# The first norm's row copy ahead of the low halves, paired column tiles in the gated feed-forward, and two-matmul products from its fifth group on

## The chip, the cores and the metric

One NeuronCore of a Trainium2 chip runs the whole program. The metric is the device time of one execution in microseconds (us). The kernel before took 830.42 us (median of 3 runs, 828.53 to 830.56). A profile is one further execution on the same kind of core, recorded by the hardware.

Engines: TensorE (PE in the rows; PEld is its weight load), VectorE (DVE), ScalarE (ACT), GpSimd (POOL) and SyncE (SP, here only a DMA queue). Each works through its own instructions strictly in order; an instruction that waits holds up all that stand behind it on that engine.

## The reference

Two layers over 256 positions of width 1024, in float32. Per layer:

```
h = rmsnorm(x)
qkv of three attention branches, gates = split(h @ w_in)
m = sum_i sigmoid(gate_i) * (attention_i(...) @ w_branch[i]);  x += m @ w_out
h = rmsnorm(x)
u = causal depthwise conv3(h @ w_up) + conv_b        # three taps along the positions
x += (silu(u_a) * u_v) @ w_down                      # u_a, u_v: the halves of u, 2816 columns each
```

A last rmsnorm ends it. The attention branches are a sliding window with sinks (A), stick-breaking (B) and a block-sparse one (C).

## The kernel before

**Split operands.** Every float32 operand of a large product is kept as a high half (rounded to the matmul's input format, by an ACT copy, tile `whi` for weights) and a low half (the remainder, by a DVE subtraction, tile `wlo`); `split` (L270) makes both. A product of a 128x128 block of weights with 256 positions is `three` (L351): high x high, high x low, low x high, each 256 columns wide into one PSUM half bank. `two` (L358) does the same work with 2 matmuls: the high half of the weights against both halves of the activations laid side by side (512 columns), then the low half of the weights against the high half of the activations (256 columns). It leaves two sums of 256 columns in the PSUM tile, which someone has to add up.

**Weights.** They come as pieces of 128x2048 (1 MB) by DMA on SP into 4 `raw` buffers and are split in two cuts of 1024 columns (`weights`, L260). There are 6 buffers each for `whi` and `wlo`, so three pieces; ACT can write a high half only once PE has finished with the cut that used the buffer six cuts earlier. One piece holds two column tiles of 128 outputs (f = 0 and 1), one in each cut, with 8 products per tile.

**Norms.** A norm isn't applied to x ahead of the product that needs it. The product starts on x times the gain (tile `xg`), and its results are scaled by 1/rms afterwards. Meanwhile the sum of squares goes through PE (L306), DVE (`var`, L309), POOL (a power, `rn`, L311) and PE again (L318), and DVE copies the result, a row of 256 scales, from PSUM into `rb` (L321). From `rb` DVE makes the scaled activations `hs` (L347, L273, L344), which the products behind use. In the first norm of a layer, q and k of branch B are computed from `xg` and scaled by `rb` (L645, 8 instructions: tiles `blk`, first q and then k); PE reads the last of them for the first logits of branch B (matmuls `at<-blk`).

**Feed-forward.** 11 groups (i = 0 to 10). In each, part a = 0 (towards silu) and part a = 1 (towards the value) take one piece of weights and give two column tiles each: 4 tiles x 8 products. `conv` (L761) makes of each tile's PSUM sum one ACT instruction (bias and the tap of the present position, L769) and two DVE instructions (the other two taps, L770 and L771). Then ACT takes silu, DVE multiplies, and ACT and DVE split the product into the gate tile `gT[i]`, tile by tile. The tiles of group 0 and the first part of group 1 are computed from `xg` and multiplied by `rb` first (L766). PSUM has 4 banks called `at` and 4 called `mm`; part 0 takes two of the first, part 1 two of the second (group 10 takes `at` for both). In layer 0 the down projection then runs output tile by output tile over k = 0 to 21, with k = 20 and 21 read from `gT[10]`; in layer 1 it runs over k outermost, and k = 18 to 21 come last.

**What sets the order.** PE's instructions are issued in the order of the code; side tasks (a norm's small matmuls, the attention) are put between by a clock that adds up columns. The order on ACT, DVE and POOL is set by the scheduler of the framework, which may move instructions past one another. `issue_after` holds an instruction back until another one of the order has been issued. Before, the low halves of the piece for k of branch B (n, c = 1, 0) are held back behind POOL's power in that way.

## Time and profile before

| | |
|---|---|
| runs | 830.42 us median (828.53 to 830.56) |
| profiled execution | 830.54 us, span 828.4 us |
| TensorE busy | 816.3 us, 99% of the span |
| VectorE busy | 670.9 us (81%) |
| ScalarE busy | 537.4 us (65%) |
| granted TensorE clock | 0.997 over the span |
| chain that ended last | PE 90%, DVE 4%, issue 4%, ACT 1% |

The span is what the profiler recorded from the first to the last instruction; the execution's own time is 2.1 us longer. A line of the page that groups instructions gives their total busy time, the mean of one, and the time that the engine stood idle in front of them. A matmul's own duration in a row overlaps its neighbours', so the pace of a row of matmuls is read from their starts.

### The profile page before, as it was taken

How to read it: one execution, taken by the hardware profiler on the slowest of the kernel's cores; microseconds unless marked ns; L12 is line 12 of the kernel's file. 1: busy time of each engine (PE TensorE's matmuls, PEld its weight loads, DVE VectorE, ACT ScalarE, POOL GpSimd, SP SyncE). 2: the span in 40 equal slices, each digit the busy share in tenths (PEclk: the TensorE clock that was granted, in tenths of full speed). 3: DMA queues.
4: the chain of work that ended last, by engine and by line, in shares of the span. 5: the costliest groups of instructions: out<-in, count | busy, mean ns of one | idle time of the engine just before them, and what ended most of it. 6: DMA issues, size and time to landing. Idle time of an engine off the chain costs nothing.

```text
span 828.4 us, 15607 instructions
## 1 busy us (share of the span) xinstructions
PE 816.3 (99%) x6268; PEld 768.9 (93%) x6268; DVE 670.9 (81%) x1205; ACT 537.4 (65%) x892; POOL 14.0 (2%) x17
## 2 busy tenths in 40 slices
PE   8999999999999999999999999999999999999996
PEld 6978899999999999999999889999999999999885
DVE  6878899677699999876658889896668999988543
ACT  7677569565567776665546777686556686766442
POOL 0100000000000000000000000000000100000000
PEclk9999999999999999999999999999999999999999
DMA  9754443555554676555565441544654566555611
GB/s 352 262 198 153 153 154 106 193 197 178 193 187 170 203 230 208 189 195 203 197 203 203 136 170 51 205 154 157 209 200 147 212 217 215 204 199 203 203 51 51
DMA packets 22631, 151.43 MB, mean 183 GB/s; under 512 B 2656, under 2 KB 3424, under 8 KB 4896
## 3 DMA queue, kind: packets, MB, share of 16 engines
q1 hardware_dynamic: 21744, 148.97, 51.3%
q8 instruction: 49, 0.80, 0.4%
q10 hardware_dynamic: 576, 0.69, 0.3%
q0 software_dynamic: 240, 0.79, 0.2%
q14 instruction: 22, 0.18, 0.1%
HBM read 149.39 MB, written 1.05 MB: 182 GB/s over the span
## 4 chain that ended last, share of the span: by engine, by line
PE 90%; DVE 4%; issue 4%; ACT 1%; POOL 0%; POOLq 0%; ACTq 0%
PE mm L181 67%; PE at L181 20%; PE at L185 2%; DVE wlo L273 1%; ACT blk L546 0%; ACT whi L271 0%; DVE blk L645 0%; DVE half L347 0%; POOL gx L217 0%; PE mm L185 0%; POOL rn L311 0%; DVE blk L559 0%; DVE half L396 0%; PE at L318 0%; DVE half L397 0%
## 5 line engine op out<-in xcount | busy, mean ns | idle before, releaser
L273 DVE TENSOR_TENSOR wlo<-raw,whi 128x1024 fp32r<-128x1024 f32 (+1 forms) x291 | 341.0, 1179 | 100.1 <-ACT whi L271 99.5
L271 ACT ACTIVATE whi<-raw 128x1024 fp32r<-128x1024 f32 (+1 forms) x291 | 294.1, 1020 | 169.9 <-PE mm L181 138.8
L181 PE MATMUL mm<-hs,whi 128*128 128x256 f32 (+1 forms) x1152 | 228.1, 294 | 0.0
L181 PEld LDWEIGHTS mm<-hs,whi 128*128 128x128 f32 x1152 | 181.9, 191 | 6.2 <-issue 0.9
L181 PE MATMUL mm<-hs,wlo 128*128 128x256 f32 x672 | 184.3, 274 | 0.0
L181 PE MATMUL mm<-blk,whi 128*128 128x256 f32 (+1 forms) x742 | 166.2, 312 | 0.1
L181 PE MATMUL mm<-blk,wlo 128*128 128x256 f32 x496 | 135.8, 274 | 0.0
L181 PEld LDWEIGHTS mm<-blk,whi 128*128 128x128 f32 x742 | 121.9, 191 | 7.8 <-DVE blk L273 0.6
L181 PEld LDWEIGHTS mm<-hs,wlo 128*128 128x128 f32 x672 | 129.0, 192 | 0.0
L181 PE MATMUL at<-hs,whi 128*128 128x256 f32 x640 | 108.5, 276 | 0.0
L181 PEld LDWEIGHTS at<-hs,whi 128*128 128x128 f32 x640 | 97.0, 192 | 0.0
L181 PEld LDWEIGHTS mm<-blk,wlo 128*128 128x128 f32 x496 | 95.2, 192 | 0.0
L181 PE MATMUL mm<-whi,hs 128*128 128x512 f32 (+1 forms) x320 | 94.7, 369 | 0.0
L181 PE MATMUL at<-hs,wlo 128*128 128x256 f32 x320 | 88.0, 275 | 0.0
L181 PEld LDWEIGHTS mm<-whi,hs 128*128 128x128 f32 x320 | 59.1, 192 | 8.3 <-issue 0.3
L181 PEld LDWEIGHTS at<-hs,wlo 128*128 128x128 f32 x320 | 61.4, 192 | 0.0
L181 PE MATMUL mm<-wlo,hs 128*128 128x512 f32 (+1 forms) x160 | 57.9, 362 | 0.0
L181 PE MATMUL mm<-whi,blk 128*128 128x512 f32 x176 | 52.5, 379 | 0.0
L181 PE MATMUL mm<-xg,whi 128*128 128x256 f32 x256 | 43.6, 276 | 0.0
L181 PEld LDWEIGHTS mm<-xg,whi 128*128 128x128 f32 x256 | 39.0, 192 | 0.1
L181 PEld LDWEIGHTS mm<-whi,blk 128*128 128x128 f32 x176 | 33.3, 189 | 4.7
L181 PE MATMUL mm<-xg,wlo 128*128 128x256 f32 x128 | 35.2, 275 | 0.0
(132 smaller groups left out, 1100.3 us busy)
## 6 DMA issues: line engine op xcount, KB each, us to landing
raw<-in_wpack SPq DMA_DIRECT2D x138, 1024.0 KB, 4.9
raw<-in_wpack SPq DMA_DIRECT2D x3, 512.0 KB, 8.8
gx<-in_x POOLq DMA_DIRECT2D x3, 256.0 KB, 7.0
out<-blk SPq DMA_DIRECT2D x2, 312.0 KB, 2.3
raw<-in_wpack SPq DMA_DIRECT2D x2, 256.0 KB, 5.7
xe<-in_gain_out SPq DMA_DIRECT2D x1, 512.0 KB, 3.7
out<-blk ACTq DMA_DIRECT2D x2, 200.0 KB, 2.6
mkt<-in_masks SPq DMA_DIRECT2D x1, 320.0 KB, 7.8
```

Of the source, the lines that this page charges most:

```text
L181: return nc.tensor.matmul(out, lhsT, rhs, **kw)
L185: nc.tensor.transpose(out, in_, ident)
L271: a = nc.scalar.activation(hi, src, AF.Copy)
L273: return a, nc.vector.tensor_tensor(lo, src, hi.bitcast(F32), OP.subtract)
```

## The change

Five edits:

1. `weights` notes its high-half instructions in `highs`. The low halves of k's first piece are held back behind the row copy `rb` (`st["copy"]`) and no longer behind POOL's power. The two ACT copies of v (`vB`) are held back behind the last high half of that piece.
2. In the feed-forward, the two column tiles of a part share one 512-wide tile `u`; the taps of both are issued in turn (tap 1 of both, tap 0 of both). Silu, the product and the split are one 512-wide instruction each per group, in place of two 256-wide ones.
3. From i = 4 on (7 groups of 11), each product is `two` and no longer `three`. The two sums are added up by an ACT copy of the second one into a `quarter` tile (L770 of the new kernel) and a DVE addition (L771 there), and bias and taps read that.
4. `half` has 7 buffers and no longer 5, `quarter` 4 and no longer 8.
5. At the very start the first piece of weights comes in DMAs of 1, 1 and 2 blocks of 512 columns, where it was 1, 2 and 1.

```diff
--- before.py
+++ after.py
@@ -162,11 +162,11 @@
         return v.rearrange("p (h i) -> p h i", h=2) if len(v.shape) == 2 else v.rearrange("p a (h i) -> p a h i", h=2)
 
     def half(n=512):
-        t = tp.tile([128, 512], F32, name="half", tag="half", bufs=5)
+        t = tp.tile([128, 512], F32, name="half", tag="half", bufs=7)
         return t[:, :n]
 
     def quarter():
-        return tp.tile([128, S], F32, name="quarter", tag="quarter", bufs=8)
+        return tp.tile([128, S], F32, name="quarter", tag="quarter", bufs=4)
 
 
 
@@ -215,7 +215,7 @@
     for q, a, b in ((nc.scalar, 0, 1), (nc.scalar, 1, 2), (nc.gpsimd, 2, 4), (nc.gpsimd, 4, 6), (nc.gpsimd, 6, 8)):
         c = slice(NG + a * S if a else 0, NG + b * S)
         q.dma_start(gx[:, c], x[:, c])
-    for i, a, b in ((0, 0, 1), (0, 1, 3), (0, 3, 4), (1, 0, 2), (1, 2, 4)):
+    for i, a, b in ((0, 0, 1), (0, 1, 2), (0, 2, 4), (1, 0, 2), (1, 2, 4)):
         c = slice(a * 512, b * 512)
         nc.sync.dma_start(first[i][:, c], wpack[0, i, :, c])
 
@@ -254,6 +254,8 @@
         return gx[:, i * KT + k : i * KT + k + 1]
 
 
+    highs = []
+
     def new_cut():
         return [wp.tile([128, 1024], F32R, name=n, tag=n) for n in ("whi", "wlo")]
 
@@ -264,7 +266,7 @@
         w = [new_cut() for _ in range(2)]
         for a in range(0, 2048, n):
             hi, lo = (q[:, a % 1024 : a % 1024 + n] for q in w[a // 1024])
-            split(hi, lo, r[:, a : a + n], after)
+            highs.append(split(hi, lo, r[:, a : a + n], after)[0])
         return lambda a, n: [q[:, a % 1024 : a % 1024 + n] for q in w[a // 1024]]
 
     def split(hi, lo, src, after=None):
@@ -308,7 +310,7 @@
         v = sp_.tile([128, 2], F32, name="var", tag="var")
         nc.vector.tensor_scalar(v, p[:, 0:2], 1.0 / D, EPS, op0=OP.mult, op1=OP.add)
         rn = sp_.tile([128, 2], F32, name="rn", tag="rn")
-        st["power"] = nc.gpsimd.tensor_tensor(rn, v, mhalf.to_broadcast([128, 2]), OP.pow)
+        nc.gpsimd.tensor_tensor(rn, v, mhalf.to_broadcast([128, 2]), OP.pow)
         return rn
 
     def spread(rn):
@@ -318,14 +320,13 @@
             nc.tensor.matmul(p[:, t * 128 : t * 128 + 128], rn[:, t : t + 1].to_broadcast([128, 128]), ident, start=True,
                              stop=True, skip_group_check=True)
         rb = np_.tile([128, S], F32, name="rb", tag="rb")
-        nc.vector.tensor_copy(rb, p[:, :S])
-        return rb
+        return rb, nc.vector.tensor_copy(rb, p[:, :S])
 
     def norm_scales(st, wait, gap, scaling=None):
         yield wait
         st["col"] = scales(st)
         yield gap
-        st["row"] = spread(st["col"])
+        st["row"], st["copy"] = spread(st["col"])
         if scaling is not None:
             st["scaled"] = scaled(scaling, st["row"])
 
@@ -626,8 +627,12 @@
             d = f3(blk())
             for c in range(2):
 
-                w = ahead if l == 0 and pc == 2 else weights(l, pc, after=st["power"] if (n, c) == (1, 0) else None)
+                w = ahead if l == 0 and pc == 2 else weights(l, pc, after=st["copy"] if (n, c) == (1, 0) else None)
                 pc += 1
+                if (n, c) == (1, 0):
+                    with tc.issue_after(highs[-1].ins):
+                        for t in range(2):
+                            nc.scalar.activation(vB[:, t, :], vps[t], AF.Copy, scale=rn[:, t : t + 1])
                 ps = [(at if n == 0 and c == 1 else mm)() for _ in range(2)]
                 if n == 0 and c == 0:
                     tn = spawn(norm_scales(st, NORM[0], NORM[2] if l else NORM[3]))
@@ -639,8 +644,6 @@
                 if n == 0 and c == 1:
                     finish(tn)
                     rn, rb = st["col"], st["row"]
-                    for t in range(2):
-                        nc.scalar.activation(vB[:, t, :], vps[t], AF.Copy, scale=rn[:, t : t + 1])
                 for f, p in pend:
                     nc.vector.scalar_tensor_tensor(halves(d[:, f, :]), unturn(p[:, :S]), 0.125 if n == 0 else 1.0, halves(rb),
                                                    op0=OP.mult, op1=OP.mult)
@@ -758,18 +761,23 @@
         h = st["h"]
         tn = spawn(norm_scales(st, NORM[1], NORM[3], scaling=2 * l + 1))
         gT = []
-        def conv(ps, a, i, raw):
-            for f in range(2):
-                j, p = a * NF + 2 * i + f, ps[f]
-                if raw:
+        def conv(ps, a, i, raw, both):
+            u, qs = half(), []
+            for f, p in enumerate(ps):
+                if raw or both:
                     q = quarter()
-                    nc.vector.tensor_tensor(q, p[:, :S], rb, OP.mult)
+                    if both:
+                        nc.scalar.activation(q, p[:, S:], AF.Copy)
+                    nc.vector.tensor_tensor(q, p[:, :S], q if both else rb, OP.add if both else OP.mult)
                     p = q
-                u = quarter()
-                nc.scalar.activation(u, p[:, :S], AF.Identity, scale=col(l, 88 + j), bias=col(l, 132 + j))
-                nc.vector.scalar_tensor_tensor(u[:, 1:S], p[:, 0 : S - 1], col(l, 44 + j), u[:, 1:S], op0=OP.mult, op1=OP.add)
-                nc.vector.scalar_tensor_tensor(u[:, 2:S], p[:, 0 : S - 2], col(l, j), u[:, 2:S], op0=OP.mult, op1=OP.add)
-                us.append(u)
+                j = a * NF + 2 * i + f
+                nc.scalar.activation(u[:, f * S : f * S + S], p[:, :S], AF.Identity, scale=col(l, 88 + j), bias=col(l, 132 + j))
+                qs.append(p)
+            for tap in (1, 0):
+                for f, p in enumerate(qs):
+                    j, c = a * NF + 2 * i + f, u[:, f * S + 2 - tap : f * S + S]
+                    nc.vector.scalar_tensor_tensor(c, p[:, 0 : S - 2 + tap], col(l, tap * 44 + j), c, op0=OP.mult, op1=OP.add)
+            us.append(u)
 
         ahead = None
         for i in range(11):
@@ -781,6 +789,7 @@
                 ahead = None
                 pc += 1
                 ps = [(at if a == 0 or i == 10 else mm)() for _ in range(2)]
+                both = i > 3
                 if i == 0 and a == 0:
                     gemm_b(w, 0, h, ps[0][:, :S], ks=range(7))
                     gemm_b(w, 1, h, ps[1][:, :S], ks=range(7))
@@ -788,7 +797,7 @@
                         gemm_b(w, f, h, ps[f][:, :S], ks=[7])
                 else:
                     for f in range(2):
-                        gemm_b(w, f, h, ps[f][:, :S])
+                        gemm_b(w, f, h, ps[f] if both else ps[f][:, :S])
                         if i == 0 and f == 0:
                             finish(tn)
                             rb, hs = st["row"], st["scaled"]
@@ -801,16 +810,12 @@
                 if i == 0 and a:
                     ahead = weights(l, pc)
                 for ps, a in pend:
-                    conv(ps, a, i, h is not hs)
-            for f in range(2):
-                k = 2 * i + f
-                if k % 2 == 0:
-                    gT.append(blk2())
-                sa = quarter()
-                last_silu = nc.scalar.activation(sa, us[f], AF.Silu)
-                g = quarter()
-                nc.vector.tensor_tensor(g, sa, us[2 + f], OP.mult)
-                split(*(parts(gT, k)[:, :, j, :] for j in range(2)), halves(g))
+                    conv(ps, a, i, h is not hs, both)
+            gT.append(blk2())
+            g = half()
+            last_silu = nc.scalar.activation(g, us[0], AF.Silu)
+            nc.vector.tensor_tensor(g, g, us[1], OP.mult)
+            split(*(gT[i][:, :, :, j, :] for j in range(2)), halves(f3(g)))
             if l == last and i == 3:
 
                 xe = np_.tile([128, 4096], F32, name="xe", tag="xg")

```

How the order moves, at three places. Names carry the buffer numbers of each program, so the same tile has different numbers in the two.

DVE, first norm of layer 1, before: in front of the row copy (`rb_5254`) stand the low halves of k's two pieces (raw_5293 and raw_5355).

```order
L273 TENSOR_TENSOR wlo_5296<-raw_5293,whi_5295 128x1024
L273 TENSOR_TENSOR wlo_5298<-raw_5293,whi_5297 128x1024
L273 TENSOR_TENSOR wlo_5358<-raw_5355,whi_5357 128x1024
L309 TENSOR_SCALAR var_5232<-at_5229 128x2
L273 TENSOR_TENSOR wlo_5360<-raw_5355,whi_5359 128x1024
L321 COPY rb_5254<-at_5251 128x256
L645 SCALAR_TENSOR_TENSOR blk_5153<-mm_5164,rb_5254 128x256
L645 SCALAR_TENSOR_TENSOR blk_5153<-mm_5165,rb_5254 128x256
L645 SCALAR_TENSOR_TENSOR blk_5153<-at_5224,rb_5254 128x256
```

And after: the row copy is `rb_5015`, and k's two pieces are raw_5052 and raw_5116.

```order
L311 TENSOR_SCALAR var_4993<-at_4990 128x2
L323 COPY rb_5015<-at_5012 128x256
L275 TENSOR_TENSOR wlo_5055<-raw_5052,whi_5054 128x1024
L648 SCALAR_TENSOR_TENSOR blk_4914<-mm_4925,rb_5015 128x256
L648 SCALAR_TENSOR_TENSOR blk_4914<-mm_4926,rb_5015 128x256
L648 SCALAR_TENSOR_TENSOR blk_4914<-at_4985,rb_5015 128x256
L275 TENSOR_TENSOR wlo_5057<-raw_5052,whi_5056 128x1024
L648 SCALAR_TENSOR_TENSOR blk_4914<-at_4986,rb_5015 128x256
L275 TENSOR_TENSOR wlo_5119<-raw_5116,whi_5118 128x1024
L275 TENSOR_TENSOR wlo_5121<-raw_5116,whi_5120 128x1024
```

All four low halves have moved behind the row copy, among the scalings of q (L648); in layer 0 they move in the same way. From the copy to the last scaling of k there were five low halves in either layer; after there are six in layer 0 and seven in layer 1.

DVE, layer 0, second norm, before: raw_3194 is the weights of group 2's part 0, raw_3262 those of its part 1; `wlo_3199` belongs to the second column tile.

```order
L273 TENSOR_TENSOR wlo_3199<-raw_3194,whi_3198 128x1024
L771 SCALAR_TENSOR_TENSOR quarter_3028<-quarter_3026,vec_114,quarter_3028 128x254
L770 SCALAR_TENSOR_TENSOR quarter_3034<-quarter_3032,vec_114,quarter_3034 128x255
L273 TENSOR_TENSOR wlo_3265<-raw_3262,whi_3264 128x1024
L771 SCALAR_TENSOR_TENSOR quarter_3034<-quarter_3032,vec_114,quarter_3034 128x254
L812 TENSOR_TENSOR quarter_3041<-quarter_3039,quarter_3028 128x256
L273 TENSOR_TENSOR wlo_3267<-raw_3262,whi_3266 128x1024
L273 TENSOR_TENSOR blk_3038<-quarter_3041,blk_3038 128x2x128
L812 TENSOR_TENSOR quarter_3047<-quarter_3045,quarter_3034 128x256
L766 TENSOR_TENSOR quarter_3101<-at_3051,rb_2953 128x256
L273 TENSOR_TENSOR wlo_3346<-raw_3343,whi_3345 128x1024
```

And after: the weights of group 2's part 0 are raw_3176.

```order
L275 TENSOR_TENSOR wlo_3179<-raw_3176,whi_3178 128x1024
L817 TENSOR_TENSOR half_3037<-half_3037,half_3025 128x512
L779 SCALAR_TENSOR_TENSOR half_3092<-quarter_3093,vec_114,half_3092 128x255
L779 SCALAR_TENSOR_TENSOR half_3092<-quarter_3096,vec_114,half_3092 128x255
L779 SCALAR_TENSOR_TENSOR half_3092<-quarter_3093,vec_114,half_3092 128x254
L779 SCALAR_TENSOR_TENSOR half_3092<-quarter_3096,vec_114,half_3092 128x254
L779 SCALAR_TENSOR_TENSOR half_3163<-mm_3113,vec_114,half_3163 128x255
L275 TENSOR_TENSOR blk_3036<-half_3037,blk_3036 128x4x128
L779 SCALAR_TENSOR_TENSOR half_3163<-mm_3113,vec_114,half_3163 128x254
L779 SCALAR_TENSOR_TENSOR half_3163<-mm_3114,vec_114,half_3163 128x255
L275 TENSOR_TENSOR wlo_3181<-raw_3176,whi_3180 128x1024
L779 SCALAR_TENSOR_TENSOR half_3163<-mm_3114,vec_114,half_3163 128x254
```

The low half of that second column tile (`wlo_3181`) now stands behind the taps of group 1's part 0 (`half_3092`) and three taps of its part 1 (`half_3163`); before, it stood in front of all these. The low half of the first column tile (`wlo_3197` before, `wlo_3179` after) has moved back as well, from three rows in front of the taps of group 0 to a place behind all of them. In layer 1 the order changes in the same way.

ACT, end of the up projection of layer 0, before: `at_4464` and `at_4465` are the last two tiles, `blk_4522` is `gT[10]`.

```order
L769 ACTIVATE quarter_4514<-at_4464,vec_114 128x256
L271 ACTIVATE whi_4632<-raw_4628 128x1024
L769 ACTIVATE quarter_4518<-at_4465,vec_114 128x256
L810 ACTIVATE quarter_4523<-quarter_4446 128x256
L810 ACTIVATE quarter_4529<-quarter_4450 128x256
L271 ACTIVATE whi_4680<-raw_4678 128x1024
L271 ACTIVATE blk_4522<-quarter_4525 128x2x128
L271 ACTIVATE blk_4522<-quarter_4531 128x2x128
L654 ACT_TABLE_LOAD
L271 ACTIVATE whi_4682<-raw_4678 128x1024
```

And after: the last two tiles are `at_4243` and `at_4244`, `gT[10]` is `blk_4290`.

```order
L273 ACTIVATE whi_4393<-raw_4389 128x1024
L774 ACTIVATE half_4277<-quarter_4278,vec_114 128x256
L770 ACTIVATE quarter_4282<-at_4244 128x256
L816 ACTIVATE half_4291<-half_4220 128x512
L657 ACT_TABLE_LOAD
L774 ACTIVATE half_4277<-quarter_4282,vec_114 128x256
L273 ACTIVATE whi_4441<-raw_4439 128x1024
L273 ACTIVATE whi_4443<-raw_4439 128x1024
L273 ACTIVATE blk_4290<-half_4291 128x4x128
```

The table load for the next layer stood behind the whole of `gT[10]` and now stands between silu and the last tile's bias, and two high halves of weights stand in front of the high half of `gT[10]`. On DVE, in the same place, one more low half (`wlo_4444`) stands in front of the low half of `gT[10]`.

## Rows read from the trace of the kernel before

**Rows 1.** page, part 1: busy time, share of the span, instructions

```profile
PE 816.3 (99%) x6268; PEld 768.9 (93%) x6268; DVE 670.9 (81%) x1205; ACT 537.4 (65%) x892; POOL 14.0 (2%) x17
```

**Rows 2.** waits of PE: total us, times, longest

```profile
PE at L181 <- DVE blk L645: 1.8, 1, 1.8
...
PE mm L181 <- ACT whi L271: 0.9, 1, 0.9
```

**Rows 3.** windows: length, busy us (instructions) by engine, clock, DMA

```profile
261.74:272.46 10.72, 10.72 (x99) 10.72 (x98) 10.72 (x21) 8.74 (x16) 0.00 (x0) 1.00 0.76 258
...
336.78:347.50 10.72, 10.72 (x99) 10.72 (x98) 9.56 (x17) 7.35 (x13) 0.00 (x0) 1.00 0.59 196
```

**Rows 4.** chain: start us, us, what; layer 0's up and down projection

```profile
261.74 5.36 PE at L181 x48
...
358.22 73.53 PE mm L181 x470
```

**Rows 5.** timeline of PE, two-matmul products: start us, us, what

```profile
369.85 0.38 PE L181 MATMUL mm<-blk,whi 128*128 128x512 f32 x1
...
372.80 0.38 PE L181 MATMUL mm<-blk,whi 128*128 128x512 f32 x1
```

**Rows 6.** timeline, layer 0's first norm, PE and DVE

```profile
23.45 0.50 PE L306 MATMUL at<-ones,ssum 128*128 128x1 f32 x4
...
24.92 0.16 DVE L309 TENSOR_SCALAR var<-at 128x2 f32<-128x2 f32 x1
...
26.84 0.60 PE L318 MATMUL at<-fct,rn 128*128 128x128 f32 x3 [0.44 <-POOL rn L311]
...
30.21 0.42 DVE L321 COPY rb<-at 128x256 f32<-128x256 f32 x1
...
43.78 0.41 DVE L645 SCALAR_TENSOR_TENSOR blk<-mm,rb 128x256 f32<-128x256 f32 x1
```

**Rows 7.** timeline, layer 1's first norm, DVE and PE

```profile
434.69 0.42 DVE L321 COPY rb<-at 128x256 f32<-128x256 f32 x1 [0.70 <-PE at L318]
...
436.15 1.87 DVE L347 SCALAR_TENSOR_TENSOR half<-gx,rb 128x256 f32<-128x256 f32 x4
...
448.76 0.42 DVE L645 SCALAR_TENSOR_TENSOR blk<-mm,rb 128x256 f32<-128x256 f32 x1 [0.34 <-PE mm L181]
...
449.30 1.16 PE L181 MATMUL at<-blk 64*128 64x128 f32 x16
```

**Rows 8.** timeline of DVE, layer 0's second norm

```profile
253.55 0.44 DVE L766 TENSOR_TENSOR quarter<-at,rb 128x256 f32<-128x256 f32 x1
...
253.88 1.23 DVE L273 TENSOR_TENSOR wlo<-raw,whi 128x1024 fp32r<-128x1024 f32 x1
...
259.41 1.22 DVE L273 TENSOR_TENSOR wlo<-raw,whi 128x1024 fp32r<-128x1024 f32 x1
```

**Rows 9.** timeline of DVE, a late group of the up projection

```profile
320.96 0.48 DVE L770 SCALAR_TENSOR_TENSOR quarter<-at,vec,quarter 128x255 f32<-128x255 f32 x1
...
321.47 0.48 DVE L771 SCALAR_TENSOR_TENSOR quarter<-at,vec,quarter 128x254 f32<-128x254 f32 x1
...
321.87 1.22 DVE L273 TENSOR_TENSOR wlo<-raw,whi 128x1024 fp32r<-128x1024 f32 x1
...
323.00 0.48 DVE L770 SCALAR_TENSOR_TENSOR quarter<-at,vec,quarter 128x255 f32<-128x255 f32 x1
```

**Rows 10.** groups of equal shape: busy us, mean ns, idle before

```profile
L769 ACT ACTIVATE quarter<-quarter,vec 128x256 f32<-128x256 f32 x12 | 7.2, 597 | 3.6 <-DVE quarter L766 3.4
...
L724 ACT ACTIVATE blk<-mm,vec 128x256 f32<-128x256 f32 x48 | 21.9, 459 | 0.0
...
L473 ACT ACTIVATE half<-half 128x512 f32<-128x512 f32 x12 | 7.5, 625 | 0.2
```

**Rows 11.** timeline, end of layer 0's up projection, ACT and DVE

```profile
362.58 1.28 ACT L654 ACT_TABLE_LOAD   x1
...
363.16 0.75 DVE L273 TENSOR_TENSOR blk<-quarter,blk 128x256 fp32r<-128x256 f32 x2
```

## Prediction

> **What bounds the kernel now.** I read the busy times first: PE is busy for 816.3 us, 99% of the span, and no other engine comes near [rows 1]. So an edit pays only if it takes work from PE or a wait of PE away, and it costs only where it makes PE wait. The waits of PE are the next view: one of 1.8 us on DVE and 0.9 us at the start [rows 2]; a third, of 0.44 us on POOL, stands in the first norm [rows 6]. The last is the table of windows over the up projection, because two edits put work on DVE and ACT there. In group 2 of layer 0 DVE is busy for all of its 10.72 us, still working off the second norm; by group 7 it needs 9.56 us and ACT 7.35 us [rows 3]. DVE thus has about 1.2 us to spare per late group, and nothing to spare in the early ones.

> The reader is to see in these rows that PE sits at its limit with the other engines just ahead of it. What decides is whether the rearranged DVE and ACT still arrive in time at three places.

> **PE's work.** A product of three matmuls takes 5.36/16 = 0.335 us (48 matmuls in a row [rows 4]). One of two takes 0.328 us: nine of them lie between the two starts, (372.80 - 369.85)/9 [rows 5]. Edit 3 changes 7 groups x 32 products x 2 layers = 448 products, at 0.0073 us each: **-3.3 us**, all of it on the path as long as PE has no new wait.

> [...]

> **First norm, layer 0.** Before, the sums are out of PE at about 23.95, but `var` starts at 24.92, behind two low halves; the copy starts at 30.21, and the last scaling of k at 43.78 [rows 6]. PE's waits of 0.44 us (ahead of the row matmuls at 26.84 [rows 6]) and 1.8 us (for that scaling [rows 2]) hang on these. After, no low half of k stands in front of `var` or the copy. `var` comes 0.9 us earlier, and with it the power that PE waited 0.44 us for; so PE runs the row matmuls at 26.4, and the copy starts some 0.55 us later, at 26.95. From the copy to the last scaling lay 13.57 us with five low halves between; now there are six. One more takes 1.13 us (321.87 to 323.00 [rows 9]). The last scaling starts at 26.95 + 13.57 + 1.13 = 41.65 and ends near 42.1. PE wanted it 1.8 us before 44.25, and 0.44 us earlier than that now: at 42.0. A low half for branch C's first product also comes about 0.2 us late. So of 2.2 us of waits some 0.3 stay: **-1.9 us**.

> **First norm, layer 1.** Here no wait was there to remove: the copy starts at 434.69, directly behind PE, and the last scaling of k starts at 448.76, when PE has just delivered the tile [rows 7]. The copy stays where it is, DVE having idled ahead of it, but seven low halves lie behind it now. DVE's work from the copy to the last scaling is 7 x 1.13 (low halves) + 9 x 0.335 (copy and scalings, a pitch like 253.55 to 253.88 [rows 8]) + 6 x 0.45 (436.15, four in 1.87 [rows 7]) + 3 x 0.6 + 2 x 0.4 (the rest of `hs`) = 16.2 us, so it ends near 450.95. The last quarter of the 16 logit matmuls that start at 449.30 and take 1.16 us [rows 7] wants it at 450.15. **+1.0 us** with the handover, between 0.4 and 1.4.

> **Group 2's second tile, each layer.** In layer 0, PE starts group 2's part 0 at 261.74 [rows 4]; its second tile begins 8 x 0.335 later, and the low half of its weights is wanted two matmuls on, at 264.64. Before, that low half ran at 259.41 [rows 8]. After, it stands behind all taps of group 0, those of group 1's part 0 and three more. DVE is full from 253.55 on, at the same work up to there. In front of `wlo_3181` then stand 6 multiplications by the row (x 0.335 = 2.0), the last three of `hs` (1.4), 15 taps (x 0.39 = 5.85), one low half (1.13), one 512-wide product and one 512-wide low half of the gate tile (0.6 each): 11.6 us, to 265.15. With its own 1.22 us it ends at 266.4, and at 266.9 if DVE waits twice for ACT, whose bias for the second tile stands behind a high half there. PE waits for 1.7 to 2.2 us; I take 2.0. Layer 1 has the same distances from copy to group 2: **+4.0 us** for both. The bounds per layer are 0 (ACT and DVE overlap more than I see) and 3.

> **End of the up projection, layer 0.** The down projection starts at 358.22 [rows 4], and k = 20 follows after 20 x 0.328 = 6.56 us; layer 1 needs these k only at its end. Before, the last low half of `gT[10]` ended at 363.91, 5.7 us after the start [rows 11]. After, the chain behind the last matmul is, on ACT: a high half (0.97), the bias of the tile before (0.55), the new copy (0.46 at most [rows 10]), silu (0.63 [rows 10]), the table load (1.28 [rows 11]), the last bias (0.6): 4.4. On DVE: two taps (0.9), a low half (1.13), the product (0.65), another low half (1.13), the low half of `gT[10]` (0.7, two 256-wide ones take 0.75 [rows 11]): 9.0 with handovers. PE waits 9.0 - 6.56 = **+2.4 us**. The bounds are 0 (load and extra low half out of the chain: 6.6) and 4.

> [...]

> **What I cost at nothing.** DVE in groups 4 to 10: four low halves (4.5), eight taps, no longer in dependent pairs (0.40 in place of 0.51 apart [rows 9]: 3.2), four additions (1.35), product and low half (1.2 to 1.3): 10.3 us against 10.49 of PE. ACT: 7.35 plus four copies of 0.46 is 9.2. Both stay below PE, and weights are split some 9 us ahead; if this cover goes, see the fourth rival. The smaller `quarter` pool: two per part, so two parts in flight, which is what DVE's order asks for. The start: block 1's weights come earlier, block 2's later; ACT was waiting for x. Between -0.9 (PE's wait goes [rows 2]) and +0.6; I take 0.

> **Sum.** -3.3 - 1.9 + 1.0 + 4.0 + 2.4 = +2.2. Against the profiled execution's 830.54 us (0.1 above the median, so one and the same here): **832.7 us**.

> **Rivals.**
> - *Group 2 in time.* If DVE reaches `wlo_3181` by 263.4 in layer 0 and alike in layer 1, the 4.0 us vanish: -1.8, 828.7 us, not slower. For it: the taps in turn are quicker than in pairs, and before, this low half was ready 4 us ahead. Against: DVE had no gap there at all, and 2 us are missing.
> - *Neither group 2 nor `gT[10]` late.* -4.2, 826.3 us. For it: only orders were read, and 6.6 against 6.56 us is nearly in time without the load. Against: the load stands in the order.
> - *The products gain little.* If two matmuls on `hs` in these tiles keep the pace of three, 3.3 us don't come: 836.0 us. Against: the gates of the second half use the same form on the same tile.
> - *DVE becomes the bound of groups 4 to 10.* If DVE's instructions don't overlap, four of 1.22, eight of 0.48, four of 0.44 and two of 0.7 make 11.8 us, 1.3 over PE; after 7 groups DVE is 9 us late, which weights ahead cover but `gT[10]` in layer 0 doesn't: 842 us. The point is 10.49 us per group. Against: successive starts lie closer than a duration [rows 9]. [...]

> **Chances.** My forecast 0.6, the first rival 0.14, the second 0.08, the third 0.08, the fourth (or part of it) 0.10. The forecast's own range is 830.5 to 835. Differences within 0.3% (2.5 us) can't be told from none. 832.7 lies just inside, so the forecast splits: 0.02 faster, 0.33 same, 0.25 slower. The first rival gives 0.04 faster and 0.10 same, the second 0.08 faster; the third and fourth are slower. Together 0.14 faster, 0.43 same, 0.43 slower. The range reaches down into the second rival and up to the third: 827.5 to 836.5.

> **What would show it.** PE's waits on a low half (`wlo`) of about 2 us near 264 and 669; one on `gT[10]` some 6.5 us after the down projection of layer 0 starts; one of 1 us at layer 1's first logits, and at layer 0's none above 0.4; 16 products in 5.24 us from group 4 on. I am wrong if PE waits nowhere in group 2, if ACT loads its table behind the last bias, or if DVE is late by more each group.

## The result and the profile after

The changed kernel takes 834.97 us (median of 6 runs, 831.64 to 836.61), the kernel before 829.57 us (6 runs, 828.53 to 830.56): a ratio of 1.0067, 95% interval 1.0051 to 1.0084, so it is slower, and above the 832.7 us forecast. The profiled execution took 836.61 us (span 834.8); it is the slowest of the six. Its busy times come first, then the waits of PE: what it waited for, total us, times, longest.

```profile
PE 817.6 (98%) x5820; PEld 757.1 (91%) x5820; DVE 683.4 (82%) x1217; ACT 550.5 (66%) x904; POOL 14.9 (2%) x17
```

```profile
PE at L181 <- DVE wlo L275: 4.1, 2, 2.1
PE mm L181 <- DVE blk L275: 2.2, 1, 2.2
...
PE at L181 <- DVE blk L648: 0.6, 1, 0.6
```

The three long ones by themselves (rows of PE; the last figure is the idle time in front, in us):

```profile
263.49 0.38 PE L181 MATMUL at<-hs,wlo 128*128 128x256 f32 x1 [2.02 <-DVE wlo L275]
...
366.05 0.64 PE L181 MATMUL mm<-blk,whi 128*128 128x512 f32 x1 [2.23 <-DVE blk L275]
...
675.46 0.38 PE L181 MATMUL at<-hs,wlo 128*128 128x256 f32 x1 [2.12 <-DVE wlo L275]
```

These are the waits that the prediction named: a low half in group 2 of each layer, `gT[10]`, and the last scaling of k in layer 1. The 1.8 us of [rows 2] and the 0.44 us of [rows 6] are gone. PE is busy 1.3 us longer than in [rows 1], though it has 3.3 us of matmuls less. The windows show one reason (length, busy us of PE, PEld, DVE, ACT, POOL, then the granted clock, DMA share, GB/s):

```profile
262.40:263.49 1.09, 0.01 (x1) 0.01 (x1) 1.09 (x2) 1.09 (x2) 0.00 (x0) 1.00 0.00 0
...
264.50:265.50 1.00, 1.00 (x7) 1.00 (x7) 1.00 (x3) 0.15 (x1) 0.00 (x0) 0.50 0.49 123
...
366.05:368.00 1.95, 1.95 (x7) 1.67 (x8) 0.42 (x1) 0.00 (x0) 0.00 (x0) 0.55 0.85 206
```

```profile
677.00:679.28 2.28, 2.28 (x12) 2.28 (x12) 2.28 (x4) 0.81 (x2) 0.00 (x0) 0.50 0.92 366
```

Behind each of the three waits of 2.0 to 2.2 us PE runs at half its clock (0.50; 0.55 in the window that begins with the first matmul behind the wait). Each such stretch lasts 3.41 us in the trace. In it a product on `gT`, 768 columns in two matmuls, takes 0.64 us (starts at 366.70 and 367.34 us) in place of 0.328 [rows 5]; so half of the work of that time is lost, 1.7 us. The 1.2 GHz of the expectations below is this pace, 768 columns in 0.64 us or 1.2 per ns: an estimate, with one column counted per cycle. Before, there is one such stretch, behind the 1.8 us wait. The window in the trace of before:

```profile
45.20:48.60 3.40, 3.40 (x9) 2.68 (x8) 2.01 (x4) 2.04 (x4) 0.00 (x0) 0.50 1.02 405
```

The stretch does not follow every wait in every execution (the traces of e3 and e10 below each have two waits of 2.0 to 2.1 us and one stretch), and that spreads the runs: those of the changed kernel took 836.5 us at a mean clock of 0.991, 834.9 to 835.1 at 0.993 to 0.995, 831.64 at 0.999; those of before about 830.4 or about 828.6, so that its median depends on which are more among them.

From group 4 on two matmuls per product in place of three bring what was expected, as the chain of work that ended last shows (16 products of a tile pair, start and us; the first line is the last pair with three):

```profile
278.55 5.36 PE mm L181 x48
283.91 5.24 PE at L181 x32
```

The two traces side by side, by the time at which PE begins the same place of the program (the last column leaves out 1.7 us for each stretch at half the clock):

| PE begins | before | after | shift in this stage | predicted | measured without the clock |
|---|---|---|---|---|---|
| sums of the first norm, layer 0 | 23.45 | 24.08 | +0.6 | 0 | +0.6 |
| up projection, layer 0 | 239.22 | 236.23 | -3.6 | -1.9 | -1.9 |
| second part of group 2 | 267.10 | 267.83 | +3.7 | +2.0 | +2.0 |
| down projection | 358.22 | 357.27 | -1.7 | -1.65 | -1.7 |
| sums of the first norm, layer 1 | 431.92 | 435.13 | +4.2 | +2.4 | +2.5 |
| up projection, layer 1 | 644.08 | 648.11 | +0.8 | +1.0 | +0.8 |
| group 3 | 677.14 | 685.17 | +4.0 | +2.0 | +2.3 |
| down projection, layer 1 | 764.64 | 771.00 | -1.7 | -1.65 | -1.7 |

The sum is +6.4 us of span: 3.0 by the terms of the prediction (2.2 foretold), and 3.4 by three stretches at half the clock where there was one.

### The profile page after: what moved, and what is told of

It is laid out like the page before. It is cut to its first block, busy times and chain, and to the rows that moved or that the text cites. A ratio compares the mean times of both kernels' runs of the same rounds, so it can differ in the third digit from the quotient of the medians.

```text
span 834.8 us, 14623 instructions
## 1 busy us (share of the span) xinstructions
PE 817.6 (98%) x5820; PEld 757.1 (91%) x5820; DVE 683.4 (82%) x1217; ACT 550.5 (66%) x904; POOL 14.9 (2%) x17
## 4 chain that ended last, share of the span: by engine, by line
PE 87%; DVE 7%; ACT 2%; issue 1%; DMA 1%; SPq 0%; POOLq 0%; POOL 0%; ACTq 0%
PE mm L181 66%; PE at L181 20%; DVE wlo L275 2%; PE at L185 1%; DMA raw<-in_wpack 1%; DVE half L348 1%; ACT blk L547 1%; ACT whi L273 1%; ACT half L774 0%; DVE hs L275 0%; DVE blk L560 0%; DVE half L397 0%; DVE half L398 0%; DVE blk L648 0%; DVE half L779 0%
## 5 line engine op out<-in xcount | busy, mean ns | idle before, releaser
L181 PEld LDWEIGHTS mm<-hs,whi 128*128 128x128 f32 x960 | 160.6, 191 | 11.2 <-issue 0.9
L181 PE MATMUL mm<-blk,whi 128*128 128x256 f32 (+1 forms) x742 | 168.0, 314 | 2.3 <-DVE blk L275 2.2
L181 PE MATMUL at<-hs,whi 128*128 128x512 f32 (+1 forms) x384 | 109.2, 354 | 0.0
L181 PEld LDWEIGHTS at<-hs,whi 128*128 128x128 f32 x384 | 69.8, 196 | 6.6
L779 DVE SCALAR_TENSOR_TENSOR half<-quarter,vec,half 128x255 f32<-128x255 f32 (+1 forms) x136 | 63.0, 479 | 4.1 <-ACT half L774 3.3
L774 ACT ACTIVATE half<-quarter,vec 128x256 f32<-128x256 f32 x68 | 39.9, 595 | 17.6 <-DVE quarter L771 17.4
```

Source lines behind the costliest of these rows:

```text
L181: return nc.tensor.matmul(out, lhsT, rhs, **kw)
L774: nc.scalar.activation(u[:, f * S : f * S + S], p[:, :S], AF.Identity, scale=col(l, 88 + j), bias=col(l, 132 + j))
L779: nc.vector.scalar_tensor_tensor(c, p[:, 0 : S - 2 + tap], col(l, tap * 44 + j), c, op0=OP.mult, op1=OP.add)
```

## The experiments

Ratios are to the kernel before, run beside it on the same chip, with their 95% intervals. As the median of the kernel before moves between such sets (828.89 to 830.43 us), the ratios are what to compare by.

| run | us, median | ratio | PE's waits in the up projections and at `gT[10]` |
|---|---|---|---|
| e1 order in group 2 | 831.91 | 1.0026 (1.0016 to 1.0036) | 0.8, 3.5, 0.8 |
| e2 table load later | 832.55 | 1.0036 (1.0022 to 1.0049) | 2.1, 1.6, 2.0 |
| e3 order at the end | 830.51 | 1.0005 (0.9997 to 1.0014) | 2.1, 0, 2.1 |
| e4 waits filled | 831.90 | 1.0029 (1.0018 to 1.0039) | 0.2, 0.6, 0.2 |
| e5 = e1 + e3 | 827.86 | 0.9976 (0.9968 to 0.9985) | 0.9, 0.8, 0.8 |
| e6 = e5, layer 1 old | 827.57 | 0.9977 (0.9968 to 0.9985) | as e5 |
| e7 edit 3 alone | 841.76 | 1.0144 (1.0125 to 1.0163) | 3.6, 8.1, 0 |
| e8 edit 1 alone | 826.92 | 0.9971 (0.9960 to 0.9982) | 0, 0, 0 |
| e9 = e5 and three edits | 824.52 | 0.9937 (0.9924 to 0.9949) | 0, 0, 0 |
| e10 without edit 3 | 834.64 | 1.0061 (1.0048 to 1.0075) | 2.0, 0, 2.0 |

**e4: the waits filled.** Is it PE's standing idle that brings the low clock?

```diff
+                        for _ in range(17 if (i, a, f) == (2, 0, 1) else 0):
+                            nc.tensor.matmul(ps[1][:, S:], still[:, :128], still[:, :S], start=True, stop=True, ...)
...
+                    if j == 20:
+                        idle = mm()
+                        for _ in range(9):
+                            nc.tensor.matmul(idle, still[:, :128], still, start=True, stop=True)
```

> PE gets matmuls without use in front of the three waits (17 of 256 columns ahead of group 2's second tile in each layer, 9 of 512 columns ahead of the 21st product of the down projection; about 1.8 to 1.9 us each); the tile waited for comes at the same time as in the changed kernel. Theory: the clock falls because PE stood idle; with PE busy through the waits the three stretches of 3.41 us at 1.2 GHz go and the data waits are hidden by the filling: 831 to 832 us, granted clock 0.997 or above. Rival: the clock falls (or the matmuls slow down) for another reason, as the load of DMA or the engines together: 834.5 to 837 us, clock 0.991 to 0.995.

The waits of PE for the low halves, and a window at the place where the clock was halved:

```profile
PE at L181 <- DVE wlo L275: 0.4, 2, 0.2
```

```profile
264.00:268.00 4.00, 4.00 (x39) 4.00 (x37) 4.00 (x6) 2.76 (x5) 0.00 (x0) 1.00 0.79 260
```

No stretch is left in the trace up to PE's last matmuls (mean granted clock 0.997 over the span, 0.991 in the changed kernel), and the runs lie within 831.76 to 832.19 us. The first tile that PE waits for comes no earlier (263.54 us in place of 263.49), yet 3.1 us of the median are gone: the theory holds. What is left, a ratio of 1.0029 or 2.4 us, is close to the +2.2 that the prediction added up from waits and matmuls.

**e1: the order in group 2.** The raised priority covers the whole fetching of this piece, so on ACT its high halves move forward together with the low halves on DVE.

```diff
-                w = ahead or weights(l, pc, n=1024 if i else 512)
-                ahead = None
+                with tc.high_priority(offset=100) if (i, a) == (2, 0) else nullcontext():
+                    w, ahead = ahead or weights(l, pc, n=1024 if i else 512), None
```

> Both low halves of group 2's first part are raised in the order of VectorE, in front of the taps of group 1's first part, in either layer; all else stays. Theory: the waits of 2.02 us (263.49) and 2.12 us (675.46) come from this order alone, and each brought a stretch of 3.41 us at 1.2 GHz behind it, which costs 1.7 us more. Both go: -4.1 us of waits and some -3 of clock, 827.5 to 829.5 us, and the granted clock rises to 0.996 or above. Rival 1: VectorE has no gap in group 2, so the lateness only moves to the next tile (a wait of 1 us or more of PE between 245 and 285): 832 to 835 us. Rival 2: the waits go but the clock falls all the same: 830.5 to 831 us, clock 0.991 to 0.995.

All three missed, rival 1 by the place: the two waits shrank to 0.8 us each, at the next tiles, and the lateness moved, but farther than group 2. PE's waits are now these:

```profile
PE mm L181 <- DVE blk L275: 3.5, 1, 3.5
PE mm L181 <- DVE wlo L275: 1.8, 3, 0.8
```

In layer 0 the waits sum up to 0.8 + 3.5 = 4.3 us, as in the changed kernel (2.02 + 2.23). What was taken from group 2 came back at `gT[10]`, where e1's one stretch at half the clock now follows (0.50 from 365.4 to 368.8 us). (That the sums are equal is partly chance: PE goes on behind `gT[10]` at 364.21 us in place of 366.05, about the one stretch that went.) Only layer 1, which needs its `gT[10]` last, kept the 1.3 us. A reason stands in the changed kernel's trace of DVE, the products of two successive gate tiles (start, us):

```profile
321.43 0.68 DVE L817 TENSOR_TENSOR half<-half 128x512 f32<-128x512 f32 x1
...
331.78 0.69 DVE L817 TENSOR_TENSOR half<-half 128x512 f32<-128x512 f32 x1
```

DVE takes 10.35 us for a group and PE 10.48: the 10.3 us that the prediction worked out. It catches up 0.13 us per group, where it could catch up about 1 us before [rows 3]. So a backlog from the second norm can be carried to the end of the projection; this is read from the rows, and no run tests it by itself.

**e2 and e3: the end of the up projection.** e2 holds the table load behind the high half of `gT[10]`; e3 also holds the low halves of the down projection's third piece behind its low half (the second hunk).

```diff
-            split(*(gT[i][:, :, :, j, :] for j in range(2)), halves(f3(g)))
+            last_cut = split(*(gT[i][:, :, :, j, :] for j in range(2)), halves(f3(g)))
...
-            with tc.issue_after(last_silu.ins):
+            with tc.issue_after(last_cut[0].ins):
```

```diff
-                        w = weights(l, pc)
+                        w = weights(l, pc, after=last_cut[1] if j == 32 else None)
```

> The load of ScalarE's table is held back behind the high half of gT[10]; VectorE's order stays. Theory: the load (1.28 us, at 359.56) stands in the chain to gT[10], so PE's wait of 2.23 us shrinks to 0.9 to 1.5 us, the rest being the two low halves of weights on VectorE: 832 to 834.2 us (the lower end if the clock no longer falls behind the shorter wait). Rival: VectorE's order sets the end, and the wait stays at 2 us or more: 835 us.

> As e2, and the low halves of the third piece of the down projection are held back behind the low half of gT[10]. Theory: with the load and the low halves out of the chain gT[10] is ready 6 to 6.5 us after the down projection starts, PE's wait of 2.23 us goes, and the stretch at 1.2 GHz behind it too: 831 to 832.7 us. Rival: the low halves that were held back are late for the 33rd product (10.5 us after the start), a new wait of 1 us or more there: 833 to 835 us.

In e2, the last instructions of DVE up to `gT[10]`, for which PE waits 1.6 us, are these:

```profile
361.71 1.22 DVE L275 TENSOR_TENSOR wlo<-raw,whi 128x1024 fp32r<-128x1024 f32 x1
362.85 0.68 DVE L817 TENSOR_TENSOR half<-half 128x512 f32<-128x512 f32 x1
363.65 1.23 DVE L275 TENSOR_TENSOR wlo<-raw,whi 128x1024 fp32r<-128x1024 f32 x1
364.79 0.69 DVE L275 TENSOR_TENSOR blk<-half,blk 128x512 fp32r<-128x512 f32 x1
```

The load cost 0.64 us of the wait (2.23 to 1.59), half of its 1.28: with it out of the way DVE's own work sets the end. In e3 that work goes, too:

```profile
360.91 0.69 DVE L817 TENSOR_TENSOR half<-half 128x512 f32<-128x512 f32 x1
362.29 0.69 DVE L275 TENSOR_TENSOR blk<-half,blk 128x512 fp32r<-128x512 f32 x1 [0.69 <-ACT blk L273]
362.90 3.49 DVE L275 TENSOR_TENSOR wlo<-raw,whi 128x1024 fp32r<-128x1024 f32 x3
```

The wait is gone, and the three low halves that now follow are in time. e2 falls inside its range, and e3's 830.51 us lies half a microsecond below its own.

**e5 and e6.** e5 is e1 and e3 together. e6 adds, for layer 1, the old hold of k's low halves.

```diff
-                w = ... weights(l, pc, after=st["copy"] if (n, c) == (1, 0) else None)
+                w = ... weights(l, pc, after=st["power" if l else "copy"] if (n, c) == (1, 0) else None)
```

> The orders of e1 and e3 together. In layer 0, e1's waits of 0.8 and 3.5 us sum up to the 4.25 us of the changed kernel (2.02 and 2.23): the lateness of VectorE was only moved to gT[10]. Theory: it is VectorE's work from the row copy to gT[10] that is too long for PE, and e3 took the load and four low halves (4.5 us) out of it, of which it needed 2.2; so what e1 moves there now finds room, and no wait is longer than 0.8 us: e3's shortest runs (829.0 us, without a stretch at 1.2 GHz) less 2 x 1.3, 826.4 us (826 to 827.5), clock 0.998 or above. Rival: gT[10] is bound by ScalarE's chain behind the last matmul, and PE, which comes 3 us earlier, waits for it again by 1 us or more: 828 to 830 us.

> As e5, and in layer 1 alone k's low halves are held back behind POOL's power again and not behind the row copy (the first edit stays in layer 0). Theory: the first norm of layer 1 lost 0.9 us by the change (0.61 of it as the wait for the last scaling of k), and gets it back: 0.5 to 1 us less than e5. Rival: more low halves now stand in front of the variance in layer 1 (five, where there were two), so the power and the copy come late and PE waits ahead of the row matmuls: equal to e5 or up to 2 us more.

e5 lands between theory and rival: behind the program's first matmuls no wait is longer than 0.9 us, and no stretch at half the clock is left before the end (mean granted clock 0.999), but 0.8 us at `gT[10]` stay. There the trace shows DVE waiting for ACT:

```profile
358.50 1.00 DVE L779 SCALAR_TENSOR_TENSOR half<-quarter,vec,half 128x255 f32<-128x255 f32 x2 [1.02 <-ACT half L774]
...
360.93 0.69 DVE L275 TENSOR_TENSOR blk<-half,blk 128x512 fp32r<-128x512 f32 x1 [0.70 <-ACT blk L273]
```

Behind PE's last matmul it is now the chain through ACT that counts, as the rival said. e6 gets back only 0.3 us, less than its theory and more than its rival. In layer 1 PE no longer waits for the scaling, but again for the power:

```profile
PE at L320 <- POOL rn L313: 0.4, 1, 0.4
```

**e7: edit 3 alone on the kernel before.**

```diff
-                        gemm_b(w, f, h, ps[f][:, :S])
+                        gemm_b(w, f, h, ps[f] if i > 3 else ps[f][:, :S])
...
+                    if both:
+                        nc.scalar.activation(q, p[:, S:], AF.Copy)
+                    nc.vector.tensor_tensor(q, p[:, :S], q if both else rb, OP.add if both else OP.mult)
```

> The kernel before with the third edit alone: two matmuls in place of three from group 4 on, with the copy and the addition, tiles gated one at a time, the old orders. Theory: PE saves 3.3 us, but VectorE needs 9.56 + 4 x 0.335 = 10.9 us per group against PE's 10.48, and is 2.9 us later after seven groups; in layer 0 PE waits 2 to 3.5 us for gT[10], in layer 1, which needs it last, not at all: 827.5 to 829.5 us, with a stretch at 1.2 GHz in part of the runs. Rival: VectorE's instructions overlap enough (10.4 us or less per group), gT[10] is in time and the whole saving stays: 825 to 826 us.

It costs 12 us, where a gain of some 1 us was expected: theory and rival both missed. The waits of PE, then from DVE's rows the products of two successive groups with a low half between them, then a high half of ACT:

```profile
PE mm L181 <- DVE blk L273: 8.1, 1, 8.1
PE at L181 <- DVE quarter L768: 3.6, 1, 3.6
```

```profile
325.88 0.43 DVE L814 TENSOR_TENSOR quarter<-quarter 128x256 f32<-128x256 f32 x1
...
331.29 1.23 DVE L273 TENSOR_TENSOR wlo<-raw,whi 128x1024 fp32r<-128x1024 f32 x1 [0.28 <-ACT whi L271]
...
338.98 0.43 DVE L814 TENSOR_TENSOR quarter<-quarter 128x256 f32<-128x256 f32 x1
```

```profile
332.81 1.06 ACT L271 ACTIVATE whi<-raw 128x1024 fp32r<-128x1024 f32 x1 [0.80 <-PE mm L181]
```

The gate tiles follow each other every 13.1 us, against PE's 10.48. In DVE's order five low halves lie in this stretch, while a group has four, and they come at PE's pace: four of the five wait 0.22 to 0.28 us for their high half, which ACT makes only when PE has freed the buffer. The expectation of 10.9 us per group left out the fifth low half (1.13) and these waits (1.04). So the lag grows by 2.6 us a group, until PE meets a tile that DVE has not read, and `gT[10]`. This is the time of the prediction's fourth rival (842 us) and one of its places, but not its reason: DVE's instructions still start inside the one before (at 338.06 us in one that runs for 0.48 us from 337.67), and DVE is busy for only 9.6 of 10.48 us. In the changed kernel four low halves lie between two products and a group takes 10.35 us; of its edits the second is the one that reorders these instructions, though no run has the second and third alone.

**e10: the changed kernel without edit 3** (`both = i > 11`).

> The changed kernel with three matmuls per product in all groups (without the third edit). Theory: the order in group 2 is the second edit's, so the waits of 2.0 and 2.1 us stay, with their stretches at 1.2 GHz in most runs; VectorE has 1.35 us less to do per group, so gT[10] is in time (-2.2 us), and PE has its 3.4 us of work back: 833 to 836 us, thus no gain of the third edit as it was made. Rival: the waits in group 2 come from the third edit and go with it: 829 to 831 us.

As expected. The 3.4 us more of matmuls and the wait at `gT[10]` that goes, with its stretch, weigh about the same, so edit 3 as made brought nothing that shows (1.0061 against 1.0067). The waits in group 2 stay:

```profile
PE at L181 <- DVE wlo L275: 4.1, 2, 2.0
```

**e8: edit 1 alone on the kernel before** (its lines are those of the change).

> The kernel before with the first edit alone. Theory: in layer 0 the wait of 1.8 us for k's last scaling goes and that of 0.44 us for the power, in layer 1 0.9 us come in, and the stretch at 1.2 GHz that followed the 1.8 us in part of the runs goes: 827.3 to 828 us, runs closer together (clock 0.999 in all). Rival: the gain in layer 0 belongs to the other edits, too (the smaller pools, the start): a wait of 1 us or more stays at k's last scaling, 828.5 to 830 us.

826.92 us, with runs within 826.81 to 827.12: a little lower than expected. In layer 0 the last scaling of k starts 2.3 us earlier than in [rows 6], and PE does not wait for it; in layer 1 the 0.6 us come in (DVE's row, then PE's):

```profile
41.45 0.41 DVE L648 SCALAR_TENSOR_TENSOR blk<-mm,rb 128x256 f32<-128x256 f32 x1
```

```profile
446.78 0.49 PE L181 MATMUL at<-blk 64*128 64x128 f32 x4 [0.60 <-DVE blk L648]
```

**e9: e5 with three more edits.**

```diff
-    for i, a, b in ((0, 0, 1), (0, 1, 2), (0, 2, 4), (1, 0, 2), (1, 2, 4)):
+    for i, a, b in ((0, 0, 1), (0, 1, 3), (0, 3, 4), (1, 0, 2), (1, 2, 4)):
...
-                with tc.high_priority(offset=100) if (i, a) == (2, 0) else nullcontext():
+                with tc.high_priority(offset=100) if i == 2 else nullcontext():
...
-                both = i > 3
+                both = 3 < i < (11 if l else 10)
```

> As e5, with three more edits: the low halves of both parts of group 2 are raised (not only of its first part), the last group of layer 0 has three matmuls per product again (no copy and addition in the chain to gT[10]), and the first weights come in the old pieces. Theory, from e5's 827.86 us: the two waits of 0.9 and 0.8 us at group 2's second part go (-1.7), that of 0.8 us for gT[10] goes at the price of 0.24 us of PE work (-0.6), and the old pieces give back 0.5 us (PE is at the sums of the first norm at 23.3 to 23.5 us in the three kernels with them, at 23.8 to 24.1 in the six without): 825 us (824.5 to 826). Rival: ScalarE, whose high halves these low halves need, is as full as VectorE in group 2, and the waits stay: 826.3 to 827.5 us.

The fastest of all, 824.52 us, at the lower end of what was expected: 5.9 us under the kernel before by the medians and 5.2 by the ratio, 10.5 us under the changed one. What each of the three edits brings was not run by itself, nor what two matmuls per product are worth in this order. By the ratios e8, edit 1 alone, has 2.4 of the 5.2 us. All waits of PE that are left:

```profile
PE at L227 <- DVE ones L247: 1.2, 1, 1.2
PE at L181 <- DVE blk L648: 0.6, 1, 0.6
PE mm L181 <- ACT whi L273: 0.4, 1, 0.4
PE mm L181 <- ACT xg L289: 0.3, 1, 0.3
PE mm L181 <- DVE wlo L275: 0.2, 1, 0.2
PE at L185 <- DVE blk L575: 0.2, 1, 0.2
```

## Why the prediction was right, and where it was not

- **The sign and the places were right, the size too small**: +2.2 us foretold, +6.1 measured between the two profiled executions (836.61 and 830.54). That the median of 834.97 us still lies below 836.5, and just below the forecast's own 835, is luck: the room up to there was meant for products that gain little, and the missing term below fell into it.
- **The missing term is the clock.** Each wait was priced at its length. A wait of about 2 us cost 3.7, since 1.7 us of work were lost in the stretch behind it at a granted clock of 0.50. Three such waits stand where one stood: +3.4 us. With the start's +0.6 that makes up the 3.9 us by which the sum fell short, but for 0.1. The trace of before showed it, in the windows behind the 1.8 us wait, which the prediction did not open. e4 takes that term away alone; e5 takes it away with the waits, e1 and e3 in part.
- **Products**: -3.3 foretold, -3.4 measured (16 in 5.24 us, in place of the 5.36 of [rows 4]).
- **First norm**: layer 0 -1.9 as foretold, layer 1 +0.8 for +1.0. In layer 0 the agreement is in part chance: the 0.3 us of waits that were to stay went as well (neither e8's trace nor the changed kernel's has one there), and the changed kernel loses 0.4 us again in the attention, in front of matmuls at 112.45 and 117.61 us, for a reason that was not followed.
- **Group 2**: 2.0 foretold, 2.02 and 2.12 measured. e10 shows that the third edit does not bring it, e8 that the first does not; the order of the second is left. From the row copy to the late low half DVE takes 17.3 us; by the prediction's times, with the copy at 248.04 us before, it is 17.1 to 17.6. What it did not have is that ACT is full there, too: from 254.43 to 260.42 us the chain that ended last runs over ACT, with a table load of 1.28 us. e1 moves both engines' halves, so the two are not told apart.
- **`gT[10]`**: 2.4 foretold, 2.23 measured (the prediction's terms on ACT add up to 4.5 and not 4.4, which leaves nothing of its 9.0 for handovers). The load is in the chain (e2), and so are the low halves of the next weights (e3). What the prediction missed is that this wait and group 2's are not independent: in e1 what leaves the one place is paid at the other.
- **DVE in groups 4 to 10**: 10.3 us foretold, 10.35 measured; the fourth rival's terms add up to 11.9 us and not 11.8. To cost that at nothing was half right: DVE keeps up, but with only 0.13 us a group over to work off a backlog.
- **The start**: costed at 0 with +0.6 as the upper end, for which the prediction gives no row, and +0.6 it was. PE's wait of 0.9 us for `whi` [rows 2] did go, but one of 1.1 us for `xg` stands in its place in this trace (0.4 before). PE reaches the sums of the first norm at 23.33 to 23.63 us in the four kernels with the old pieces (before, e7, e8, e9) and at 23.84 to 24.16 in the eight with the new. What the order of the DMAs changes inside was not tried.

## What to carry to other kernels

Price a wait of the bounding engine with what its clock does behind it (here 1.7 us more for each of three waits of 2.0 to 2.2 us): look at the granted clock of the windows after the waits that are there already. Where the second engine has only 0.1 us to spare in 10.5, as here, moving one late tile forward may only move the lateness, so take work out of the chain to the last consumer before reordering it. An edit that saves work on the full engine by giving some to the next one (e7) first needs room there, in the order as well as in the busy time.
